# Probabilities' parts in four narrower buffers with products a step later, a shifted ring of accumulators, one gate multiplication on GpSimd, and closing scalings by pairs, in a two-layer encoder trunk

## The chip, the cores and the metric

The kernel runs on one core of a Trainium2 chip. The core has TensorE (PE: matrix products into the banks of PSUM, and transposes, which are products with an identity), VectorE (DVE), ScalarE (ACT), GpSimd (POOL) and SyncE (SP, which here issues DMAs). Each works through its own list of instructions in order and waits on semaphores for the others. The metric is the device time of one execution in microseconds (us), smaller is better.

## The reference

One sequence of 1024 tokens on a grid of 16 rows of 64, width 1024, passes two layers, all in float32:

```python
for l in range(DEPTH):
    h = rmsnorm(x, norm_gain[l])
    mk, mv = jnp.split(memn @ w_mem_kv[l], 2, axis=-1)
    ...
    if l % 2 == 0:
        qa, ka, va, qb, kb, vb, qm, gate = split_cols(h @ w_in_even[e], SPLIT_EVEN)
        ya = global_gqa(...); yb = window_gqa(...); ym = memory_attn(...)
        x = x + (concat(ya, yb, ym) * silu(gate)) @ w_out_even[e]
    else:
        qc, kc, vc, qm, gate = split_cols(h @ w_in_odd[o], SPLIT_ODD)
        yc = neighborhood_attn(qc, kc, vc, rpb_c[o])
        ym = memory_attn(qm, mk, mv)
        x = x + (concat(yc, ym) * silu(gate)) @ w_out_odd[o]
return rmsnorm(x, final_norm_gain)
```

The change lies in the odd layer, but for one line of the first stage. There 16 neighbourhood heads of 64 channels attend to the keys of a few grid rows around a query's own (at most three blocks of 128 keys for a block of 128 queries), four memory heads of 128 channels to 256 memory tokens; the heads' outputs are multiplied by a gate, go through one output projection, are added to x, and a last RMS norm closes.

## The kernel before

[...]

*Stages.* The projection of the global heads' queries and keys (0 to 143 us of the profile); the even layer's attention and output projection and the odd layer's first projections (to 985); the odd layer's memory heads (to 1124); its neighbourhood heads, called near below (to 1368); the output projection with the last norm (to 1490). Tiles of SBUF come from rings: each tag has a number of buffers, and a new tile takes the place of the oldest of its tag, for which the writer waits until the old one's last reader is done. The same holds for PSUM banks (pj, tr, s, pv, sa).

*Order.* In the odd layer the order of PE's instructions is that in which the code writes them. On the other engines a scheduler puts each instruction as early as its inputs allow, by priorities that the code gives by kind (`ahead`); `issue_after` holds one back behind another.

*First stage.* `project_a` begins with nine warm-up products into one bank of the tag pj, a ring of five that the projections then use. After the last of them the first scores (bank sa) of the memory heads follow; DVE adds the last projection's halves into q (L128).

*Memory heads of the odd layer.* `mem_flips` transposes a head's probabilities into two banks; `p_parts` makes of each the high part ph by a copy on ACT and the low part pl by a subtraction on DVE (L541), both of 512 columns; `mem_pv` takes three products for each. ph and pl have three buffers each.

*Near heads.* `near` runs over 128 steps n, one for each of 16 heads and 8 blocks. A step's score is two products on PE (s), a sum with the bias and a maximum on DVE (L1111), exp on ACT (L1114), a reciprocal on DVE (L1115) and the normalisation on POOL (L1116, tile pn). At every second step two key blocks, n-6 and n-5, are transposed (`flips`: PE into a bank tr, then `p_parts` of up to 384 columns). `values(n - 7)` takes the product of one key block's ph and pl with v into the accumulators pv. Between these, `fill` takes 1930 columns' worth of products from a list: the projections of keys and gates still to come, and at the end the first part of the output projection. POOL also makes the weight parts for that (L1276 for the output projection). The output of a pair of heads is done every 16 steps; `gated_steps` (which also takes the last memory head, at the start) then spreads its gating over the following scores, one job of POOL or DVE behind a score's normalisation, and only behind scores at which no weight job is left: the second half's multiplication (L477), the first half's (L480), and for the rows that have k of 6 or more a store, a load and three subtractions on POOL (L496, L498, L501). The last pair's jobs come after the loop, when the output projection has begun (`behind_held`).

*Output projection.* The rows y and their differences are loaded again as operands; its weights are split by ACT and POOL (L1276), and for each output block six products of a kind follow.

*The end.* `finish` works on the last 512 columns in two halves: residual, squares and their sums over channels by PE, the root (DVE), its spread to rows by PE, then for eight channel blocks the scaling by row and gain: three on POOL (L1488; gains applied before), five on DVE in one instruction each with the gain, and four stores per half.

## Time and profile before

| | |
|---|---|
| median of 3 runs | 1495.13 us (1492.85 to 1495.61) |
| the profiled execution | 1492.08 us |
| its span, first to last instruction | 1490.3 us |
| granted clock, mean | 0.998 |
| PE busy | 1468.7 us, 99% of the span |
| DVE, ACT, POOL busy | 1036.9, 832.0 and 634.7 us |
| PE's last work | about 1483 us |

In the lines of the profile each row has a start and a length in us, the engine, the line of the code (L62 stands for all that goes through `Pinned`, and is told apart by its tiles), the operation, and out<-in. A matmul's end is modelled, and neighbouring ones overlap; the starts tell the rate. In square brackets stands idle time ahead of a row and what ended it. Rows of a stage table hold start and end, length, and busy time (with instructions) of PE, PE's weight loads, DVE, ACT and POOL, then the granted clock, the share of the DMA engines and GB/s.

### The profile page before, as it was taken

The numbers are of one execution on the slowest core, as the hardware profiler recorded it, in microseconds if no ns is written. First come the engines' busy times: TensorE is split into PE (matmuls) and PEld (weight loads), VectorE is DVE, ScalarE is ACT, GpSimd is POOL, SyncE is SP. The second block draws the span as 40 slices with busy tenths as digits, with TensorE's granted clock in tenths as the row PEclk, the third lists the DMA queues.
The fourth block names the chain that finished last, engine by engine and source line by source line (L and its number), as shares of the span: only waits on it lengthen the run. The fifth ranks groups of instructions, "written<-read, shape, count | busy, mean of one in ns | idle before, by whom it ended". The sixth has DMA issues, their size and how long they took to land.

```text
span 1490.3 us, 25353 instructions
## 1 busy us (share of the span) xinstructions
PE 1468.7 (99%) x8385; PEld 1272.7 (85%) x8385; DVE 1036.9 (70%) x2121; ACT 832.0 (56%) x1855; POOL 634.7 (43%) x761
## 2 busy tenths in 40 slices
PE   9999999999999999999999999999999999999997
PEld 8898888988888788888879877888988888888886
DVE  6786777677676578776677766654346877788674
ACT  7743665656655456654545444444446777676452
POOL 1223668556765746543450000002325556664354
PEclk9999999999999999999999999999999999999999
DMA  8966335434433424388653444567675578689834
GB/s 285 317 157 184 112 119 174 128 107 137 127 125 129 139 87 135 98 285 292 196 178 114 138 138 142 154 164 262 212 259 166 181 216 249 207 295 341 305 101 140
DMA packets 173859, 271.90 MB, mean 182 GB/s; under 512 B 15648, under 2 KB 96800, under 8 KB 172704
## 3 DMA queue, kind: packets, MB, share of 16 engines
q1 hardware_dynamic: 173296, 270.20, 56.4%
q8 instruction: 66, 1.08, 0.3%
q14 instruction: 65, 0.53, 0.1%
q10 hardware_dynamic: 432, 0.09, 0.0%
HBM read 174.28 MB, written 83.89 MB: 173 GB/s over the span
## 4 chain that ended last, share of the span: by engine, by line
PE 84%; DVE 6%; DMA 5%; issue 2%; ACT 2%; POOL 1%; SPq 0%; POOLq 0%; DVEq 0%; ACTq 0%
PE pj L241 15%; PE pj L62 11%; PE x L1599 6%; PE tr L132 5%; PE pv L1063 4%; PE y L1599 4%; PE pv L62 3%; PE s L62 3%; PE pj L1329 3%; PE tr L62 2%; PE sa L1329 2%; PE pv L1599 2%; PE s L1329 2%; PE sa L1030 2%; PE sa L1031 2%
## 5 line engine op out<-in xcount | busy, mean ns | idle before, releaser
L241 PE MATMUL pj<-H,wh 128*128 128x512 f32 x704 | 233.6, 412 | 0.5 <-DVE vt L312 0.2
L541 DVE TENSOR_TENSOR pl<-tr,ph 128x512 fp32r<-128x512 f32 (+2 forms) x336 | 202.2, 615 | 42.6 <-ACT ph L124 40.4
L124 ACT ACTIVATE ph<-tr 128x512 fp32r<-128x512 f32 (+2 forms) x336 | 174.3, 539 | 97.1 <-PE tr L132 80.5
L157 POOL TENSOR_SCALAR wh<-wraw 128x512 fp32r<-128x512 f32 x48 | 33.3, 696 | 277.7 <-PE x L1599 235.1
L124 ACT ACTIVATE wh<-wraw 128x384 fp32r<-128x384 f32 (+1 forms) x163 | 89.0, 554 | 107.6 <-PE pj L1329 13.4
L241 PE MATMUL pj<-H,wl 128*128 128x512 f32 x352 | 139.3, 396 | 0.0
L241 PEld LDWEIGHTS pj<-H,wh 128*128 128x128 f32 x704 | 120.8, 190 | 19.1 <-POOL wh L157 0.6
L62 PE MATMUL pj<-H,wh 128*128 128x512 f32 x384 | 121.0, 396 | 0.0
L1116 POOL TENSOR_SCALAR pn<-pn,st 128x384 f32<-128x384 f32 (+1 forms) x128 | 72.6, 568 | 113.1 <-DVE st L1115 67.5
L132 PE MATMUL tr<-ident,P 128*128 128x128 f32 x752 | 115.5, 273 | 0.9 <-DVE pl L541 0.6
L1276 POOL TENSOR_TENSOR wl<-wraw,wh 128x384 fp32r<-128x384 f32 x56 | 63.6, 1137 | 97.0 <-ACT wh L124 87.5
L1114 ACT ACTIVATE pn<-pn,st 128x384 f32<-128x384 f32 (+1 forms) x128 | 75.2, 588 | 40.7 <-DVE st L1111 40.0
L132 PEld LDWEIGHTS tr<-ident,P 128*128 128x128 f32 x752 | 88.9, 140 | 9.1 <-DVE pl L541 1.5
L1036 ACT ACTIVATE P<-sa,st 128x1024 f32<-128x1024 f32 x64 | 71.5, 1117 | 35.3 <-PE tr L132 19.1
L1038 POOL TENSOR_SCALAR P<-P,st 128x1024 f32<-128x1024 f32 x64 | 74.6, 1168 | 32.2 <-DVE st L1037 32.2
L1035 DVE TENSOR_REDUCE st<-sa 128x1 f32<-128x1024 f32 x64 | 77.6, 1218 | 8.5 <-PE sa L1031 8.0
L62 PE MATMUL s<-k,q 128*128 128x384 f32 (+1 forms) x352 | 81.3, 327 | 0.0
L241 PEld LDWEIGHTS pj<-H,wl 128*128 128x128 f32 x352 | 66.3, 188 | 15.3
L62 PE MATMUL pj<-H,wl 128*128 128x512 f32 x192 | 75.8, 395 | 0.0
L159 POOL TENSOR_TENSOR wl<-wraw,wh 128x512 fp32r<-128x512 f32 x52 | 68.6, 1323 | 9.5 <-ACT wh L124 6.6
L62 PEld LDWEIGHTS pj<-H,wh 128*128 128x128 f32 x384 | 67.0, 189 | 5.8
L848 PE MATMUL pj<-ah,H 128*128 128x256 f32 x384 | 70.5, 282 | 0.9 <-ACT H L124 0.9
(559 smaller groups left out, 4171.2 us busy)
## 6 DMA issues: line engine op xcount, KB each, us to landing
wraw<-w_o SPq DMA_DIRECT2D x52, 256.0 KB, 3.7
y<-yb SPq DMA_DIRECT2D x24, 512.0 KB, 3.5
wraw<-s SPq DMA_DIRECT2D x64, 192.0 KB, 3.7
wraw<-w_e SPq DMA_DIRECT2D x44, 256.0 KB, 3.3
k<-k SPq DMA_DIRECT2D x42, 256.0 KB, 5.1
s<-bias SPq DMA_DIRECT2D x56, 192.0 KB, 2.0
wq<-w_o SPq DMA_DIRECT2D x40, 256.0 KB, 3.3
y<-sg SPq DMA_DIRECT2D x18, 512.0 KB, 2.9
```

Source lines behind the costliest of these rows:

```text
L62: return lambda *a, **k: self.tc.keep_in_program_order(getattr(self.engine, name)(*a, **k))
L124: return self.nc.scalar.activation(out, in_, AF.Copy, scale=scale)
L132: self.turned = self.fence = self.pe.transpose(o, i, self.ident)
L241: self.pe.matmul(a[:, :n], s[:, kt % UNIT, :], m, start=(kt == 0 and i == 0), stop=(kt == KT - 1 and i == 2))
L541: self.low = nc.vector.tensor_tensor(pl[:, :n], tr[:, :n], ph[:, :n], op=OP.subtract)
L1035: nc.vector.tensor_reduce(st[:, 0:1], s, axis=AX.X, op=OP.max, negate=True)
L1036: nc.scalar.activation(pt, s, AF.Exp, bias=st[:, 0:1], accum_out=st[:, 1:2])
L1038: self.normal = nc.gpsimd.tensor_scalar(pt, pt, st[:, 2:3], 0.5, op0=OP.mult, op1=OP.mult)
L1114: nc.scalar.activation(o, o, AF.Exp, bias=st[:, 0:1], scale=-1.0, accum_out=st[:, 2:3])
L1116: self.normal = normal = nc.gpsimd.tensor_scalar(o, o, st[:, 3:4], 0.5, op0=OP.mult, op1=OP.mult)
L1329: last = nc.tensor.matmul(bank, s[:, k, :], y[3 * u + k][m][:, cols], start=start and u + k + e == 0, stop=u == 1 and k + e == 4, skip_gro ...
L1599: self.last = nc.tensor.matmul(bank, ws[s][:, k, :], b[k][m], start=start and k + i == 0, stop=k == UNIT - 1 and i == 2, skip_group_check= ...
```

## The change

- In the odd layer ph and pl get four buffers instead of three, each of 384 columns instead of 512. The memory heads' parts are made in two pieces of 256 columns, with six products instead of three.
- The near heads' `values` come one step later after their transposes (n-8 for n-7), the loop is one step longer, and the load of the next v moves from step 7 to step 8 of a pair.
- Of the two gate multiplications of a near pair, the second half's goes from DVE to POOL. Nine jobs have a `gap` of 2, the last memory head's and those of the eight pairs of near heads: eight of the instructions are issued within the loop, the last pair's behind it.
- The warm-up's products use two pj banks in turn, by which every later tile of this tag takes the next bank of its ring.
- In `finish` the gains of the channel blocks that DVE scaled are applied early, by copies on ACT; the scalings are then products of two operands, two channel blocks at a time, and the stores come in the order of the pairs 2, 3, 0, 1. Squares of the output projection take the buffers of the tag bm in place of ph.

```diff
@@ -86,2 +86,3 @@
         self.raws = []
+        self.wide, self.square_tag = 512, "ph"
         self.later_jobs = ()
@@ -476,6 +477,6 @@
             yield
-        (nc.vector if gap > 1 else nc.vector).tensor_tensor(y[:, second], y[:, second], sg[:, second], op=OP.mult)
+        (nc.gpsimd if gap > 1 else nc.vector).tensor_tensor(y[:, second], y[:, second], sg[:, second], op=OP.mult)
         for _ in range(gap):
             yield
-        (nc.vector if gap > 1 else nc.vector).tensor_tensor(y[:, first], y[:, first], sg[:, first], op=OP.mult)
+        nc.vector.tensor_tensor(y[:, first], y[:, first], sg[:, first], op=OP.mult)
         if k < 6:
@@ -536,4 +537,4 @@
         nc = self.nc
-        ph = self.st("ph", [128, 512], F32R)
-        pl = self.st("pl", [128, 512], F32R)
+        ph = self.st("ph", [128, self.wide], F32R)
+        pl = self.st("pl", [128, self.wide], F32R)
         with self.ahead("part"):
@@ -659,3 +660,4 @@
             self.flip((tr[c][:, b * 128:(b + 1) * 128], pt[:, b, c * 128:(c + 1) * 128]) for c in range(2) for b in range(4))
-        return [self.p_parts(t, 512) for t in tr]
+        n = min(512, self.wide // 256 * 256)
+        return [[self.p_parts(t[:, i:i + n], n) for i in range(0, 512, n)] for t in tr]
 
@@ -663,6 +665,7 @@
         vh, vl = (kv[:, i, :].rearrange("p (c d) -> p c d", c=2)[:, c, :] for i in (2, 3))
-        ph, pl = parts
+        n = 512 // len(parts)
         with self.ahead("pv"):
-            for e, (a, b) in enumerate(((vh, ph), (vl, ph), (vh, pl))):
-                self.pe.matmul(o, a, b, start=c + e == 0, stop=c * e == 2)
+            for i, (ph, pl) in enumerate(parts):
+                for e, (a, b) in enumerate(((vh, ph), (vl, ph), (vh, pl))):
+                    self.pe.matmul(o[:, i * n:(i + 1) * n], a, b, start=c + e + i == 0, stop=c * e == 2, skip_group_check=True)
 
@@ -964,5 +967,5 @@
         nc.scalar.activation(self.rs_m, warm.bitcast(F32)[:, :2], AF.Sqrt)
-        p = self.ps("pj")
+        p = [self.ps("pj") for _ in range(2)]
         for i in range(9):
-            nc.tensor.matmul(p, warm[:, :128], warm, start=True, stop=True)
+            nc.tensor.matmul(p[i % 2], warm[:, :128], warm, start=True, stop=True)
         w0, w1m = io["w_mem0"], io["w_mem1"]
@@ -1156,3 +1159,3 @@
 
-        for n in range(128 + 7):
+        for n in range(128 + 8):
             for f in (n - 6, n - 5) if n % 2 == 0 else ():
@@ -1177,3 +1180,3 @@
                     pair["q"] = load_q(j + 1)
-                if j < 7 and at == 7:
+                if j < 7 and at == 8:
                     pair["v"] = load_v(j + 1)
@@ -1185,6 +1188,6 @@
                     pair[j]["g"] = gate(j, ("sg", "mk")[j % 2])
-            if n >= 7:
-                values(n - 7)
-                if (n - 7) % 16 == 15:
-                    j = (n - 7) // 16
+            if n >= 8:
+                values(n - 8)
+                if (n - 8) % 16 == 15:
+                    j = (n - 8) // 16
                     self.later_jobs.append(self.gated_steps(pair[j]["g"], pair[j]["y"], yd, ROWS.index(j), 2))
@@ -1357,3 +1360,3 @@
 
-            sq = self.st("ph" if k else "vt", [128, 512])
+            sq = self.st(self.square_tag if k else "vt", [128, 512])
             nc.scalar.activation(sq, x, AF.Square)
@@ -1456,5 +1459,8 @@
         at = [xs[k // 2][:, k % 2, :] for k in range(KT)]
-        for k in range(3):
-            nc.gpsimd.tensor_scalar(at[k], at[k], gains[k], 1.0, op0=OP.mult, op1=OP.mult)
-        sq = self.st("ph", [128, 512])
+        for k in range(7):
+            if k < 3:
+                nc.gpsimd.tensor_scalar(at[k], at[k], gains[k], 1.0, op0=OP.mult, op1=OP.mult)
+            else:
+                self.copy(at[k], at[k], gains[k])
+        sq = self.st(self.square_tag, [128, 512])
         ss, rows = [self.ps("pv")[:, :16] for _ in range(2)], {}
@@ -1486,11 +1492,22 @@
             self.copy(sb, rows[h][1])
-            for k in range(3):
-                nc.gpsimd.tensor_tensor(at[k][:, c], at[k][:, c], sb, op=OP.mult)
-            for k in (4, 5, 6, 7, 3):
-                pinned.scalar_tensor_tensor(at[k][:, c], at[k][:, c], gains[k], rows[h][0], op0=OP.mult, op1=OP.mult)
+            two = lambda t: t[:, None, :].to_broadcast([128, 2, c.stop - c.start])
+            out = lambda p: nc.sync.dma_start(
+                self.io["out"][2 * p:2 * p + 2, :, 512 + c.start:512 + c.stop].rearrange("k p t -> p k t"), xs[p][:, :, c])
+            x = xs[0][:, :, c]
+            nc.gpsimd.tensor_tensor(x, x, two(sb), op=OP.mult)
+            if h == 0:
+                nc.gpsimd.tensor_tensor(at[2][:, c], at[2][:, c], sb, op=OP.mult)
+            for p in (2, 3):
+                x = xs[p][:, :, c]
+                pinned.tensor_tensor(x, x, two(rows[h][0]), op=OP.mult)
                 yield
-                if k % 2:
-                    for p in (k // 2,) if k > 3 else (0, 1):
-                        nc.sync.dma_start(self.io["out"][2 * p:2 * p + 2, :, 512 + c.start:512 + c.stop].rearrange("k p t -> p k t"),
-                                          xs[p][:, :, c])
+                out(p)
+            if h == 0:
+                pinned.tensor_tensor(at[3][:, c], at[3][:, c], rows[h][0], op=OP.mult)
+            else:
+                x = xs[1][:, :, c]
+                pinned.tensor_tensor(x, x, two(rows[h][0]), op=OP.mult)
+            yield
+            out(0)
+            out(1)
 
@@ -1499,2 +1516,3 @@
             nc.scalar.activation(sq[:, c], x3[:, c], AF.Square)
+            self.copy(x3[:, c], x3[:, c], gains[7])
         cols = [slice(0, 256), slice(256, 512)]
@@ -1860,4 +1878,5 @@
             self.alias = {"P": "k"}
-            with self.phase("l1", ("pool", "pool"), q=4, k=8, v=2, pn=8, ph=3, pl=3, sg=1, yb=2, bt=1, vt=3, bm=2,
+            with self.phase("l1", ("pool", "pool"), q=4, k=8, v=2, pn=8, ph=4, pl=4, sg=1, yb=2, bt=1, vt=3, bm=2,
                             p_s=2, p_tr=2, p_pv=2, p_pj=2):
+                self.wide, self.square_tag = 384, "bm"
                 first, begun = self.odd(wo, kvd[1], yd[1], vd, mqd, qd, gd)
```

PE, at the end of the near stage, where `fill` has no products left: the last transposes (tr), and the products of key blocks 125 and on (pv). Before:

```order
L62 MATMUL tr_3530_16274<-ident_1_63,pn_3493_16146 128x128
L62 MATMUL tr_3530_16274<-ident_1_63,pn_3506_16182 128x128
L62 MATMUL tr_3530_16274<-ident_1_63,pn_3510_16199 128x128
L62 MATMUL tr_3533_16282<-ident_1_63,pn_3506_16182 128x128
L62 MATMUL tr_3533_16282<-ident_1_63,pn_3510_16199 128x128
L62 MATMUL pv_3513_16206<-ph_3527_16259,v_3326_15544 128x384
L62 MATMUL pv_3513_16206<-pl_3528_16260,v_3326_15544 128x384
L62 MATMUL pv_3513_16206<-ph_3531_16278,v_3326_15544 128x384
L62 MATMUL pv_3513_16206<-pl_3532_16279,v_3326_15544 128x384
L62 MATMUL pv_3513_16206<-ph_3534_16285,v_3326_15544 128x256
L62 MATMUL pv_3513_16206<-pl_3535_16286,v_3326_15544 128x256
```

After, from the last row of block 126's transposes:

```order
L62 MATMUL tr_3562_16380<-ident_1_63,pn_3542_16307 128x128
L62 MATMUL tr_3565_16388<-ident_1_63,pn_3539_16293 128x128
L62 MATMUL tr_3565_16388<-ident_1_63,pn_3542_16307 128x128
L62 MATMUL pv_3551_16337<-ph_3557_16362,v_3368_15687 128x128
L62 MATMUL pv_3552_16338<-ph_3557_16362,v_3368_15687 128x256
L62 MATMUL pv_3551_16337<-pl_3558_16363,v_3368_15687 128x128
L62 MATMUL pv_3552_16338<-pl_3558_16363,v_3368_15687 128x256
L62 MATMUL pv_3552_16338<-ph_3560_16370,v_3368_15687 128x384
L62 MATMUL pv_3552_16338<-pl_3561_16371,v_3368_15687 128x384
L62 MATMUL pv_3552_16338<-ph_3563_16384,v_3368_15687 128x384
L62 MATMUL pv_3552_16338<-pl_3564_16385,v_3368_15687 128x384
```

Before, a block's products follow straight on the transposes of the last two; now the four products of the block before these (128 and 256 columns) stand between.

POOL, in the output projection, where the last pair is gated: yb is the pair's output, mk its gate and later its differences, wl the low parts of weights. Before:

```order
L501 TENSOR_TENSOR yb_3305_15480<-sg_3320_15522,yb_3305_15480 128x512
L1276 TENSOR_TENSOR wl_3562_16391<-wraw_3560_16388,wh_3561_16390 128x384
L1276 TENSOR_TENSOR wl_3574_16454<-wraw_3572_16451,wh_3573_16453 128x384
L1276 TENSOR_TENSOR wl_3580_16486<-wraw_3578_16483,wh_3579_16485 128x384
L496 TENSOR_TENSOR mk_3491_16133<-yb_3428_15925,mk_3491_16133 128x512
L498 TENSOR_TENSOR mk_3491_16133<-yb_3428_15925,mk_3491_16133 128x512
L501 TENSOR_TENSOR yb_3428_15925<-mk_3491_16133,yb_3428_15925 128x512
```

After:

```order
L502 TENSOR_TENSOR yb_3338_15591<-sg_3353_15633,yb_3338_15591 128x512
L1279 TENSOR_TENSOR wl_3595_16504<-wraw_3593_16501,wh_3594_16503 128x384
L1279 TENSOR_TENSOR wl_3607_16567<-wraw_3605_16564,wh_3606_16566 128x384
L478 TENSOR_TENSOR yb_3461_16036<-yb_3461_16036,mk_3523_16239 128x512
L1279 TENSOR_TENSOR wl_3613_16599<-wraw_3611_16596,wh_3612_16598 128x384
L497 TENSOR_TENSOR mk_3523_16239<-yb_3461_16036,mk_3523_16239 128x512
L499 TENSOR_TENSOR mk_3523_16239<-yb_3461_16036,mk_3523_16239 128x512
L502 TENSOR_TENSOR yb_3461_16036<-mk_3523_16239,yb_3461_16036 128x512
L1279 TENSOR_TENSOR wl_3619_16633<-wraw_3617_16630,wh_3618_16632 128x384
```

The multiplication (L478 of the new code) now stands between two weight parts, and the pair's three subtractions behind one weight part more; in the loop the other multiplications stand each behind a normalisation (L1116), with a normalisation following. On PE the low part that follows, which had two products of the next bank ahead of it, now has seven.

DVE, at the end, from the first half's scalings on: tr holds the row of roots, H and yb are the pairs of channel blocks. Before:

```order
L62 SCALAR_TENSOR_TENSOR yb_3549_16324<-yb_3549_16324,gain_2_65,tr_3764_17411 128x256 x2
L62 RECIPROCAL rq_v_3767_17426<-pv_3759_17351 128x2
L62 SCALAR_TENSOR_TENSOR pv_3759_17351<-pv_3759_17351,rq_v_3767_17426 128x2 x2
L62 SCALAR_TENSOR_TENSOR rq_y_3768_17427<-pv_3759_17351,rq_v_3767_17426 128x2
L62 SCALAR_TENSOR_TENSOR yb_3550_16325<-yb_3550_16325,gain_2_65,tr_3764_17411 128x256 x2
L62 SCALAR_TENSOR_TENSOR H_3544_16319<-H_3544_16319,gain_2_65,tr_3764_17411 128x256
L62 SCALAR_TENSOR_TENSOR yb_3549_16324<-yb_3549_16324,gain_2_65,tr_3769_17433 128x256 x2
L62 SCALAR_TENSOR_TENSOR yb_3550_16325<-yb_3550_16325,gain_2_65,tr_3769_17433 128x256 x2
L62 SCALAR_TENSOR_TENSOR H_3544_16319<-H_3544_16319,gain_2_65,tr_3769_17433 128x256
```

After:

```order
L62 TENSOR_TENSOR yb_3582_16437<-yb_3582_16437,tr_3797_17530 128x2x256
L62 TENSOR_TENSOR yb_3583_16438<-yb_3583_16438,tr_3797_17530 128x2x256
L62 RECIPROCAL rq_v_3800_17545<-pv_3792_17468 128x2
L62 SCALAR_TENSOR_TENSOR pv_3792_17468<-pv_3792_17468,rq_v_3800_17545 128x2 x2
L62 SCALAR_TENSOR_TENSOR rq_y_3801_17546<-pv_3792_17468,rq_v_3800_17545 128x2
L62 TENSOR_TENSOR H_3577_16432<-H_3577_16432,tr_3797_17530 128x256
L62 TENSOR_TENSOR yb_3582_16437<-yb_3582_16437,tr_3802_17552 128x2x256
L62 TENSOR_TENSOR yb_3583_16438<-yb_3583_16438,tr_3802_17552 128x2x256
L62 TENSOR_TENSOR H_3577_16432<-H_3577_16432,tr_3802_17552 128x2x256
```

Scalings by one block (twice 128x256) have become one of 128x2x256; two of them, instead of two single ones, stand ahead of the second half's reciprocal.

## The prediction

> **What bounds the kernel now.** I read the page's head first, then busy time by stage, then who waits for whom in the near stage, then the places themselves in order of time.
>
> ```profile
> span 1490.3 us, 25353 instructions
> PE 1468.7 (99%) x8385; PEld 1272.7 (85%) x8385; DVE 1036.9 (70%) x2121; ACT 832.0 (56%) x1855; POOL 634.7 (43%) x761
> ...
> 1124.00:1368.00 244.00, 240.89 (x1413) 212.17 (x1412) 191.60 (x598) 176.59 (x460) 140.26 (x193) 1.00 0.73 236
> 1368.00:1483.00 115.00, 113.78 (x535) 94.10 (x534) 74.43 (x118) 54.35 (x105) 54.39 (x48) 1.00 0.56 186
> 1483.00:1490.30 7.30, 0.30 (x3) 0.06 (x1) 2.66 (x7) 0.38 (x1) 2.80 (x5) 0.56 0.79 276
> ```
>
> TensorE (PE) is busy nearly always and the granted clock is 1.00 in the near stage (1124 to 1368), so only time in which PE waits can be won, and the 7.3 us after its last work. In the near stage DVE works 191.6 of 244 us and POOL 140.3, so neither is full. The run of this profile took 1492.08 us; the median of the timed runs is 1495.13, which is 3.05 more. I make the sum against the former and carry the difference over to the latter.
>
> ```profile
> PEld pv L62 <- DVE pl L541: 6.4, 12, 0.9
> PE pv L62 <- DVE pl L541: 2.8, 8, 0.6
> ...
> 1276.98 0.34 PE L62 MATMUL pv<-ph,v 128*128 128x384 f32 x1
> 1277.16 0.34 PE L62 MATMUL pv<-pl,v 128*128 128x384 f32 x1
> ...
> 1278.38 0.34 PE L62 MATMUL pv<-ph,v 128*128 128x384 f32 x1
> 1278.69 0.89 DVE L541 TENSOR_TENSOR pl<-tr,ph 128x384 fp32r<-128x384 f32 x2
> 1279.30 0.44 PE L62 MATMUL pv<-pl,v 128*128 128x384 f32 x1 [0.58 <-DVE pl L541]
> ```
>
> The first two lines are waits of the near stage: total, times, longest. The product with the low part pl waits for VectorE (DVE) to make it. PE's own 2.8 us understates this, since a matmul's modelled end covers part of the gap: undisturbed, the second product starts 0.18 us after the first (1276.98, 1277.16), here 0.92 us after (1278.38, 1279.30). That is 0.74 lost where the row says 0.58. The weight loads' 6.4 us in 12 waits is the better sum, and I use it.
>
> **The change, part by part.**
>
> *Values one step later, parts in four buffers.* One step is a score, a fill and a product: 244 us over 135 steps, 1.8 us. Today the even key blocks' parts are wanted one step after their transposes, the odd ones' two; the change makes it two and three. The longest wait is 0.9 us, half of the step given. In DVE's new order every pl stands behind the same score's work as before, none behind a later one, so the step is real slack. Four buffers hold the block more that lives; a buffer comes free the same number of steps before its next use as now, so no wait comes with it. The load of the next v moves a step with the values; no row has PE waiting for v.
>
> The end of the stage is different, because there the fill is used up:
>
> ```profile
> 1364.75 0.71 PE L62 MATMUL tr<-ident,pn 128*128 128x128 f32 x5
> 1365.47 0.34 PE L62 MATMUL pv<-pl,v 128*128 128x384 f32 x1
> 1365.94 0.44 PE L62 MATMUL pv<-ph,v 128*128 128x384 f32 x1
> 1366.12 0.89 DVE L541 TENSOR_TENSOR pl<-tr,ph 128x384 fp32r<-128x384 f32 x2
> 1366.73 0.44 PE L62 MATMUL pv<-pl,v 128*128 128x384 f32 x1 [0.35 <-DVE pl L541]
> ```
>
> From 1365.94 to 1366.73 are 0.79 us for a product of 0.18, from 1365.47 to 1365.94 are 0.47: 0.9 lost in all. The new order puts only block 124's four products between, about 0.45 us by the 128- and 256-column starts. So of 6.4 us I take 5.5 in the body as gone, and of the 0.9 at the end 0.4: **-5.9** (bounds -6.7, the same waits counted from start to start, and 0).
>
> *Parts of 256 columns in the memory heads.* 48 products of 512 columns become 96 of 256.
>
> ```profile
> 1042.93 0.63 PE L62 MATMUL pv<-ph,k 128*128 128x512 f32 x2
> 1043.40 0.39 PE L62 MATMUL pv<-pl,k 128*128 128x512 f32 x1
> ...
> 1474.31 0.28 PE L1329 MATMUL pj<-H,wl 128*128 128x256 f32 x1
> 1474.43 0.39 PE L1329 MATMUL pj<-H,wh 128*128 128x256 f32 x2
> ```
>
> Two 512-column products take 0.47 us from start to start, one of 256 takes 0.12: 0.235 against 0.24. That is 48 x 0.005, **0.2** at most, and I take 0: no wait of PE for these parts is listed in this stage, and the 16 more copies and subtractions lie on ACT and DVE, which have room. Below nothing it can't be.
>
> *The accumulators' ring in the first stage.* Each projection still follows the one five before it, so inside that stage nothing moves. The warm-up ends before the first operands are there. But the bank that the last projection leaves changes hands at the stage's end:
>
> ```profile
> 142.00 0.39 PE L1031 MATMUL sa<-k,q 128*128 128x512 f32 x1
> 142.55 0.68 DVE L128 TENSOR_TENSOR q<-pj,q 128x512 fp32r<-128x512 f32 x1
> 143.38 0.47 PE L1030 MATMUL sa<-k,q 128*128 128x512 f32 x1 [0.99 <-DVE q L128]
> ```
>
> Now the second score's bank is read by DVE until 143.23. In the new order this score has no wait on DVE, and the projection after it has. Four score products of 0.23 us fit between (142.23 to 143.16), so 0.2 us of the wait is left: **-0.8** (bounds -1.0 and 0).
>
> *One gate multiplication of two on GpSimd.* Nine multiplications leave DVE, eight inside the stage's loop and that of the last pair behind it.
>
> ```profile
> L1116 POOL TENSOR_SCALAR pn<-pn,st 128x384 f32<-128x384 f32 x96 | 56.8, 593 | 82.4 <-DVE st L1115 41.6 <-PE tr L62 26.5 <-PE s L62 9.2
> L496 POOL TENSOR_TENSOR sg<-yb,sg 128x512 f32<-128x512 f32 x3 | 3.9, 1288 | 0.0
> ...
> L477 DVE TENSOR_TENSOR yb<-yb,mk 128x512 f32<-128x512 f32 x5 | 3.7, 735 | 0.0
> ```
>
> On GpSimd I price one like L496, 1.29 us against DVE's 0.74. Queued behind it are the next block's normalisation (L1116) and, for it, PE's transposes four steps later (7 us). GpSimd sits idle 82 us ahead of 96 of its normalisations, 0.86 us each, and never more than one such job is given out per score, so the eight fall where no weight job stands: **0** (bounds 0 and 8 x 1.29 = 10.3).
>
> [...]
>
> ```profile
> 1374.85 0.68 DVE L128 TENSOR_TENSOR q<-q 128x512 fp32r<-128x512 f32 x1
> 1376.27 1.20 POOL L1276 TENSOR_TENSOR wl<-wraw,wh 128x384 fp32r<-128x384 f32 x1 [2.98 <-ACT wh L124]
> 1376.52 1.50 DVE L128 TENSOR_TENSOR q<-q 128x512 fp32r<-128x512 f32 x1
> ```
>
> The same subtraction takes 0.68 us alone and 1.50 beside a GpSimd subtraction. [...]
>
> *The last pair's multiplication* stands on GpSimd in line with weight parts of the output projection, and behind it a store, a load and three subtractions.
>
> ```profile
> 1376.16 0.32 SPq L491 DMA_DIRECT2D y<-yb  x1
> 1383.97 1.29 POOL L496 TENSOR_TENSOR mk<-yb,mk 128x512 f32<-128x512 f32 x1 [2.07 <-issue]
> 1388.05 2.76 POOL L1276 TENSOR_TENSOR wl<-wraw,wh 128x384 fp32r<-128x384 f32 x2
> ...
> 1391.21 0.40 PE L1342 MATMUL pv<-k,wl 128*128 128x512 f32 x1
> ```
>
> It can start when the weight part of 1376.27 is done, 1377.5, and ends at 1378.8, so the store goes 2.6 us late and the three subtractions too. The weight part behind them is then ready at about 1392.0 instead of 1389.4, where PE wants it at 1391.21. But the new order lets PE do five products more of the next bank first (1.2 us), so it is wanted at 1392.4. I take **+0.3** (bounds 0 and 2.6).
>
> *The closing scalings.*
>
> ```profile
> 1366.93 1.28 DVE L1354 TENSOR_TENSOR H<-H,pj 128x512 f32<-128x512 f32 x2
> ...
> 1480.94 0.87 DVE L62 SCALAR_TENSOR_TENSOR yb<-yb,gain,tr 128x256 f32<-128x256 f32 x2 [0.64 <-PE tr L132]
> 1481.62 4.27 POOL L1488 TENSOR_TENSOR H<-H,vt 128x256 f32<-128x256 f32 x6 [8.49 <-ACT vt L124]
> 1481.77 0.17 DVE L62 RECIPROCAL rq_v<-pv 128x2 f32<-128x2 f32 x1
> 1485.76 1.01 SPq L1494 DMA_DIRECT2D out<-H  x2
> ...
> DMA  0000000000399306999999999999999998000000
> ```
>
> GpSimd's six of 0.71 become two of 1.29 and one of 0.71: 3.3 us for 4.3. DVE's two scalings ahead of the second half's root take 1.28 instead of 0.87, so that root starts 0.4 us later; the three pairs behind it end at about 1485.5, where DVE and GpSimd end at 1485.7 and 1485.9 now. The gains move to ACT, which the stage table shows busy for 54 of the last stage's 115 us, as four copies of 512 columns and two of 256, each behind its square. The last row (40 slices of 1480 to 1490.4) says what sets the end: the DMA engines work on a first store in slices 10 to 13 (from 1482.6), have a hole, and are full from slice 15 to slice 33 (1483.9 to 1488.8): seven stores of equal size in 4.85 us, 0.69 us each. The hole of 0.5 us (a third full, empty, 0.6 full) mostly goes if the second store is issued at 1482.3 instead of 1483.05, as it would be, with DVE's first pair done. **-0.4** (bounds -0.7 and +0.4, the late root).
>
> Squares in two buffers: one square per product of 4.2 us, its sum 1.3 us; 0.
>
> Sum: -5.9 - 0.8 + 0 + 0 + 0.3 - 0.4 = **-6.8 us**, 1485.3 for the profiled run and 1488.3 for the median.
>
> **The rivals.**
>
> *The wait moves to the transposes.* A transpose needs a bank that pl frees. At the stage's end this is so (five transposes at 1364.75, just as DVE ends the parts before them), and one step more for the values gives the banks nothing. If it holds in the body too, some 5 of the 5.9 us come back: 1493.3. Against it: no line names PE's transposes of pn as waiting.
>
> [...]
>
> *The last pair's chain costs all of it.* 2.6 us once at the weight part, and as much again where the late store is loaded back: -6.8 - 0.3 + 5.2 = -1.9, 1493.2.
>
> *It doesn't do what it says*: if DVE made each pl a step later too, nothing would be won. Its order says no.
>
> **How the numbers follow.** 0.67 for the forecast, 0.13 for the transposes, 0.09 for the last pair's chain, 0.09 for GpSimd, 0.02 for the last. A measurement of this kernel can tell about 0.2%, 3.0 us. The forecast lies beyond it, two rivals within, one above: faster 0.70, same 0.18, slower 0.12. The range goes down to all good ends, -1.0 - 6.7 - 0.7 = -8.4, less another 1.7 for the spread of the runs shown (2.8 us): 1485. Up it takes in both rivals at 1493 and a part of GpSimd's: 1496.
>
> **What would show it.** Right: the waits of pv for pl in the near stage fall from 6.4 us to under 1; the wait of sa near 143 is gone; DVE's L477 rows stand on POOL at about 1.29 us. Wrong: PE's tr waits for pl or for pn from POOL; the wl of 1388 comes after PE wants it; stores that end later than now after PE's last work.

## The result and the profile after

Over seven runs of each the changed kernel took 1488.59 us (1485.98 to 1491.39), the one before 1494.25 us (1491.65 to 1495.66). The ratio is 0.9965 with a 95% interval of 0.9952 to 0.9978: 5.2 us faster (3.3 to 7.2). A second set of runs gave 0.9971 (0.9959 to 0.9984). The profiled execution took 1488.59 us, 3.5 less than that of before. The head of the profile's page, and the stage table at the same times as before:

```profile
span 1486.8 us, 25511 instructions
PE 1467.6 (99%) x8433; PEld 1274.7 (86%) x8433; DVE 1030.7 (69%) x2124; ACT 837.2 (56%) x1877; POOL 644.2 (43%) x767
...
1124.00:1368.00 244.00, 242.70 (x1432) 215.88 (x1432) 190.28 (x596) 178.46 (x466) 148.82 (x202) 1.00 0.73 238
```

POOL works 8.6 us more in this window and DVE 1.3 less. A sharper measure is the time between the same two instructions of PE, the near stage's first score of 384 columns and its last product with pl. Rows of the timeline, before and then after:

```profile
1123.03 0.51 PE L62 MATMUL s<-k,q 128*128 128x384 f32 x2
...
1367.13 0.32 PE L62 MATMUL pv<-pl,v 128*128 128x256 f32 x1
```

```profile
1124.51 0.51 PE L62 MATMUL s<-k,q 128*128 128x384 f32 x2
...
1364.01 0.32 PE L62 MATMUL pv<-pl,v 128*128 128x256 f32 x1
```

That is 244.1 us before and 239.5 after: 4.6 won in this stage. Who waits for whom in it (total, times, longest):

```profile
PE tr L62 <- DVE pl L542: 0.9, 2, 0.6
```

And three of its places in the timeline:

```profile
1279.00 0.34 PE L62 MATMUL pv<-ph,v 128*128 128x384 f32 x1
1279.18 0.34 PE L62 MATMUL pv<-pl,v 128*128 128x384 f32 x1
...
1296.76 0.52 PE L62 MATMUL tr<-ident,pn 128*128 128x128 f32 x3 [0.33 <-DVE pl L542]
...
1363.46 0.34 PE L62 MATMUL pv<-ph,v 128*128 128x384 f32 x1
1363.63 0.42 PE L62 MATMUL pv<-pl,v 128*128 128x384 f32 x1
```

No product waits for pl any more (the pair at 1279.00 is 0.18 us apart, where it was 0.92), and the waits listed for PE in this stage went from the products, 6.4 us by weight loads, to the transposes, 0.9 us (and 0.2 us for v). In the first stage the second score no longer stands before DVE is done with q:

```profile
143.63 0.40 PE L1033 MATMUL sa<-k,q 128*128 128x512 f32 x1
...
144.56 0.39 PE L1033 MATMUL sa<-k,q 128*128 128x512 f32 x1
144.89 0.68 DVE L129 TENSOR_TENSOR q<-pj,q 128x512 fp32r<-128x512 f32 x1
```

And the end of the kernel, first the timeline:

```profile
1478.23 1.28 DVE L62 TENSOR_TENSOR yb<-yb,tr 128x512 f32<-128x512 f32 x2 [0.64 <-PE tr L133]
1478.98 0.99 SPq L1494 DMA_DIRECT2D out<-yb  x2
1480.34 0.40 PE L133 MATMUL tr<-ident,rq_y 128*128 128x128 f32 x2 [1.59 <-DVE rq_y L62]
1480.58 0.38 PE L133 MATMUL pj<-ident,rq_y 128*128 128x128 f32 x2
```

Then the DMA engines' share in 40 slices of 0.26 us, from 1476.4 to 1486.8:

```profile
DMA  0000000000000499999999999999999999600000
```

The stores now run without a hole, from 1479.8 to 1485.4. PE waits 1.6 us for the second root instead of 1.2. From the near stage's last product to PE's last start are 116.7 us (115.9 before), and from there to the end of the span 6.1 (7.3 before).

The table shows three stretches of each kernel's profiled execution: the near stage as above; from there to PE's last start; from that to the end of the span. The ratio is to runs of the kernel before on the same chip.

| kernel | near | output projection | end | ratio (95%) |
|---|---|---|---|---|
| before | 244.1 | 115.9 | 7.3 | |
| changed | 239.5 | 116.7 | 6.1 | 0.9965 (0.9952 to 0.9978) |
| changed, again (e9) | 239.2 | 116.6 | 5.8 | 0.9971 (0.9959 to 0.9984) |
| products at n-7 again (e1) | 243.1 | 116.4 | 6.1 | 0.9989 (0.9980 to 0.9997) |
| both multiplications on DVE (e2) | 240.9 | 116.3 | 6.1 | 0.9971 (0.9963 to 0.9980) |
| both on GpSimd (e3) | 246.2 | 117.0 | 5.8 | 1.0008 (0.9995 to 1.0022) |
| buffers and later products alone (e4) | 241.9 | 115.9 | 7.2 | 0.9978 (0.9966 to 0.9990) |
| gating earlier (e5) | 245.6 | 117.7 | 5.8 | 0.9989 (0.9975 to 1.0004) |
| both on GpSimd and earlier (e6) | 239.6 | 117.0 | 6.1 | 0.9969 (0.9958 to 0.9980) |
| earlier, root first (e7) | 243.2 | 117.2 | 7.0 | 1.0005 (0.9994 to 1.0017) |
| earlier but for one pair (e8) | 238.7 | 116.7 | 6.1 | 0.9967 (0.9953 to 0.9981) |
| that, last pair on DVE (e10) | 239.3 | 116.3 | 6.1 | 0.9964 (0.9950 to 0.9978) |

### The profile page after: what moved, and what is told of

Its sections match the earlier page's. It is cut to its first block, busy times and chain, and to the rows that moved or that the text cites. A ratio compares the mean times of both kernels' runs of the same rounds, so it can differ in the third digit from the quotient of the medians.

```text
span 1486.8 us, 25511 instructions
## 1 busy us (share of the span) xinstructions
PE 1467.6 (99%) x8433; PEld 1274.7 (86%) x8433; DVE 1030.7 (69%) x2124; ACT 837.2 (56%) x1877; POOL 644.2 (43%) x767
## 4 chain that ended last, share of the span: by engine, by line
PE 86%; DMA 6%; DVE 3%; ACT 2%; issue 1%; SPq 1%; POOL 1%; POOLq 0%; ACTq 0%; DVEq 0%
PE pj L242 16%; PE pj L62 11%; PE x L1617 6%; PE tr L133 6%; PE pv L1066 4%; PE y L1617 4%; PE pv L62 3%; PE s L62 3%; PE pj L1332 3%; PE tr L62 3%; PE sa L1332 2%; PE pv L1617 2%; PE sa L1033 2%; PE s L1332 2%; PE sa L1034 2%; PE pj L851 2%
## 5 line engine op out<-in xcount | busy, mean ns | idle before, releaser
L160 POOL TENSOR_TENSOR wl<-wraw,wh 128x512 fp32r<-128x512 f32 x52 | 69.6, 1341 | 10.3 <-ACT wh L125 7.8
```

## The experiments

The first four expectations count the near stage from a later start, a projection product some 9 us on, to the end of its last product: 234.8 us before (from 1132.61), 231.4 after (from 1132.94). In what follows the table's count is used, and the differences are what is compared; where an expectation gives a length of the stage, its own count stands beside it.

**The later products undone (e1).**

```diff
-        for n in range(128 + 8):
+        for n in range(128 + 7):
...
-                if j < 7 and at == 8:
+                if j < 7 and at == 7:
...
-            if n >= 8:
-                values(n - 8)
-                if (n - 8) % 16 == 15:
-                    j = (n - 8) // 16
+            if n >= 7:
+                values(n - 7)
+                if (n - 7) % 16 == 15:
+                    j = (n - 7) // 16
```

> The changed kernel with values at n-7 again (and the load of v at step 7); four buffers, 256-column parts, the ring, the multiplication on GpSimd and the closing scalings stay as changed. Theory (the later products make the gain of the near stage): the stage from its first projection product to its last product with pl, 231.4 us in the changed kernel's profile and 234.8 before, goes back to 234 to 236, the waits of PE for pl in it are back at 5 to 7 us counted on the weight loads, and the time is 3 to 6 us longer than that of the changed kernel, a ratio to before of 0.999 to 1.001. Rival (the relief of DVE by GpSimd made the gain): the stage stays at 231 to 232 and the ratio at 0.9965.

The stage is 3.6 us longer (in the expectation's count 233.8 us, just short of its 234) and the time 0.9989 of before, at the lower edge of the theory's range and far from the rival's 0.9965. The waits are back, about as many and as long as before:

```profile
PEld pv L62 <- DVE pl L542: 5.9, 12, 0.8
...
PE pv L62 <- DVE pl L542: 2.6, 7, 0.5
```

What is left of the gain with the products at n-7 (243.1 against 244.1) is 1.0 us: the larger part needs the later products.

**Both multiplications on DVE (e2), and both on GpSimd (e3).**

```diff
-        (nc.gpsimd if gap > 1 else nc.vector).tensor_tensor(y[:, second], y[:, second], sg[:, second], op=OP.mult)
+        nc.vector.tensor_tensor(y[:, second], y[:, second], sg[:, second], op=OP.mult)
```

> The changed kernel with both gate multiplications on DVE. Theory (the eight cost nothing and bring nothing, the last pair's costs 0 to 0.3 us): ratio to before 0.9965 within 0.0015, stage 231 to 232 us. Rival 1 (GpSimd's multiplications hold normalisations): 3 us or more faster than the changed kernel, stage 229 or less. Rival 2 (they made the gain by relieving DVE): 3 us slower, waits of transposes or products for pl above 3 us.

```diff
-        nc.vector.tensor_tensor(y[:, first], y[:, first], sg[:, first], op=OP.mult)
+        (nc.gpsimd if gap > 1 else nc.vector).tensor_tensor(y[:, first], y[:, first], sg[:, first], op=OP.mult)
```

> The changed kernel with the first half's multiplication on GpSimd as well: eight more of 1.29 us in the near stage. Theory (GpSimd's idle time takes them): stage 231 to 232.5 us, ratio to before 0.9960 to 0.9985; only the last pair's, with its store another 1 to 2.6 us later, may cost up to 1 us. Rival (each holds a normalisation and with it PE): 8 x 1.29 = 10 us longer at the most, a ratio of 1.000 to 1.004, with waits of PE's transposes for pn.

With both on DVE the time can't be told from the changed kernel's (0.9971 against 0.9965 and 0.9971), so neither rival holds. But the profile has the stage 1.4 to 1.8 us longer than in the changed kernel's two profiles (232.8 us in the expectation's count, above its 231 to 232), nearly all of it ahead of transposes:

```profile
DVE yb L1158 <- DMA y<-yb: 5.3, 3, 2.1
...
PE tr L62 <- DVE pl L542: 2.4, 4, 1.4
```

With both on GpSimd the theory fell: 246.2 us, 6.7 more (238.1 in the expectation's count), and slower than the changed kernel by 0.43% or some 6 us. The ratio, 1.0008, lies in the rival's range; the rival's mechanism isn't there, for PE doesn't wait for normalisations:

```profile
DVE yb L1158 <- DMA y<-yb: 6.1, 3, 3.9
...
PE s L62 <- DMA k<-k: 2.6, 3, 1.0
...
PE tr L62 <- DVE pl L542: 2.3, 2, 1.8
```

DVE waits for a store. A pair's output tile yb has two buffers; the sum that closes a head (L1158) writes into the one that the pair before the last is stored from, and stands on DVE until that store has landed. Behind it on DVE stand pl, and behind these PE's transposes, for which a bank must come free. The changed kernel has the same row with 3.7 us in 3 waits. These transposes cost 2.7 us from start to start, at one place (1303.59). More, 3.7 us, was lost at another, where the last key pair's loads came late: PE stood about 2.2 us for them (the second row), and then the granted clock was low: 0.89 over the 15 us of the stage table, where the changed kernel has 1.00. The table:

```profile
1330.00:1345.00 15.00, 13.18 (x68) 11.38 (x67) 9.18 (x31) 8.17 (x22) 7.85 (x10) 0.89 1.04 350
```

**Buffers and later products alone (e4).** This is the kernel before with four buffers, the 256-column parts and the products at n-8.

> The kernel before with the four buffers of 384 columns, the 256-column parts and the products one step later alone; both multiplications on DVE, the old ring and the old closing scalings. Theory: the near stage's 3.4 us come with this alone, a ratio to before of 0.9970 to 0.9985, and the wait of sa for q (1.0 us) is there again. Rival (buffers and lag need DVE's relief): ratio 0.999 to 1.000.

The ratio, 0.9978, is as expected, but the stage is not: it is 2.2 us shorter than before where the changed kernel's is 4.6 (in the expectation's count 1.0 of the 3.4). It is also 1.0 us longer than in e2, which has the same code in this stage; e4's profile has waits of PE for v, 1.3 us, that e2's has not. So two profiles of one code can lie 1 us apart here. e4's profile has the old end (115.9, and 7.2 us behind PE) and the old wait in the first stage, which none of the kernels with the shifted ring has:

```profile
PE sa L1033 <- DVE q L129: 1.0, 1, 1.0
```

**The gating two scores earlier (e5), and this with both multiplications on GpSimd (e6).** If the chain behind the multiplications is what comes late, it can be started earlier.

```diff
-        for _ in range(gap):
-            yield
+        yield
         (nc.gpsimd if gap > 1 else nc.vector).tensor_tensor(y[:, second], y[:, second], sg[:, second], op=OP.mult)
-        for _ in range(gap):
-            yield
+        yield
         nc.vector.tensor_tensor(y[:, first], y[:, first], sg[:, first], op=OP.mult)
```

> The changed kernel with one score instead of two ahead of each of a pair's two gate multiplications, so that everything behind them (store, load, subtractions, last store) comes earlier by up to two scores. Theory (what is left of PE's waits in the near stage starts with DVE's write into yb, which waits 3.7 us in 3 waits for the store of the pair before the last, and with it the pl behind it): these waits fall below 1 us, PE's waits of tr for pl from 0.9 to under 0.3, the stage from its first 384-column score to its last product with pl is 238 to 239 us against 239.5, and the time is 0.5 to 1.5 us shorter, a ratio to before of 0.9950 to 0.9965. Rival (the transposes wait because two banks are too few): the waits of yb fall and those of tr stay, the stage is 239.5 and the ratio 0.9965.

> Both multiplications on GpSimd, and both one score earlier each. With both on GpSimd the near stage took 246.2 us, 6.7 more than in the changed kernel. Theory (what costs is the lateness of the chain behind the multiplications: the store that holds SyncE's queue, and yb's buffer): the stage goes back to 240 to 243 us and the ratio to before to 0.997 to 0.999. Rival (it is GpSimd's own time, 8 x 1.29 us that hold normalisations): the stage stays at 245 to 247 us, the ratio at 1.0008.

The second of these answers the question for GpSimd: 16 multiplications in the stage, started earlier, take 239.6 us and 0.9969. The stage is even a little under the expected 240 to 243. So GpSimd's own time is not what cost 6 us in e3; it is when the chain behind the multiplications comes. With this order PE has no wait for k and no slow clock in the stage.

The first went wrong: slower than the changed kernel (0.9989), 245.6 us. Of what the theory names, a part came. Against the changed kernel 0.5 us are won at the transposes of 1296.76; at those of 1326.68 the first three come 0.6 us earlier, but the next three wait for a pl of their own, and nothing is left. DVE's wait for the store is 1.8 us instead of 3.7 (below 1 was expected), and the transposes' waits for pl stay at 1.0 in the list (under 0.3 was expected). A new wait, once, cost more than all that was won. PE's timeline there:

```profile
1326.69 0.52 PE L62 MATMUL tr<-ident,pn 128*128 128x128 f32 x3 [0.49 <-DVE pl L540]
1330.46 0.55 PE L62 MATMUL s<-k,q 128*128 128x256 f32 x1 [3.25 <-DMA k<-k]
```

The stage table of the same place (granted clock third from the right):

```profile
1326.60:1330.40 3.80, 0.52 (x3) 0.31 (x3) 2.19 (x7) 2.18 (x7) 2.00 (x3) 0.85 1.03 230
1330.40:1334.00 3.60, 3.07 (x9) 2.52 (x10) 0.60 (x3) 0.60 (x2) 3.13 (x4) 0.50 1.03 199
1334.00:1337.00 3.00, 3.00 (x12) 2.54 (x11) 0.73 (x3) 0.71 (x2) 1.67 (x3) 0.65 1.03 378
```

And SyncE's queue:

```profile
1318.24 0.32 SPq L490 DMA_DIRECT2D y<-yb  x1
1318.61 0.75 SPq L491 DMA_DIRECT2D mk<-y  x1
1319.46 0.73 SPq L366 DMA_DIRECT2D k<-k  x1
```

In the changed kernel three of the four loads of keys came first:

```profile
1320.07 0.47 SPq L366 DMA_DIRECT2D k<-k  x1
...
1324.60 0.40 SPq L492 DMA_DIRECT2D y<-yb  x1
1325.09 0.47 SPq L367 DMA_DIRECT2D k<-k  x1
1325.61 1.32 SPq L493 DMA_DIRECT2D mk<-y  x1
```

PE stood 3.5 us, counted from start to start, for the last key pair, whose four transfers (L366, L367) came behind a store and a load of 0.5 MB each; from issue to landing they took a median of 12.0 us instead of 5.8, with the DMA engines full (share 1.03). Then PE went on at a granted clock of 0.50 for 3.6 us and of 0.65 for 3.0; by the granted clocks of the two rows behind the stall it lost about 2.8 us more (3.6 x 0.50 + 3.0 x 0.35, an estimate).

**One pair left out (e8), and the changed kernel beside it (e9).** The sixth pair's gating, whose store it was, keeps its two scores, and so does the last memory head's at the start of the stage. The new argument is their number (0: as `gap`).

```diff
-    def gated_steps(self, sg, y, yd, k, gap=1):
+    def gated_steps(self, sg, y, yd, k, gap=1, lead=0):
...
-        for _ in range(gap):
+        for _ in range(lead or gap):
...
-        for _ in range(gap):
+        for _ in range(lead or gap):
...
-                    self.later_jobs.append(self.gated_steps(pair[j]["g"], pair[j]["y"], yd, ROWS.index(j), 2))
+                    self.later_jobs.append(self.gated_steps(pair[j]["g"], pair[j]["y"], yd, ROWS.index(j), 2, 2 if j == 5 else 1))
```

> The gating two scores earlier for all near pairs but the sixth, whose store and load stood ahead of the last key pair's four loads on SyncE's queue. Theory (that kernel lost its gain, and more, by this alone: the keys landed late, PE stood 3.5 us and then ran at half its clock): no wait of PE for k, the granted clock 1.00 from 1320 to 1345 us, the near stage from its first 384-column score to its last product with pl 238 to 239.3 us (239.5 in the changed kernel, 245.6 with all pairs earlier), a ratio to before of 0.9955 to 0.9970. Rival (earlier gating loads the DMA engines everywhere): the wait for k stays or moves to another pair, stage over 242, ratio 0.998 or more.

> The changed kernel once more, for a comparison with the others of this call: a ratio to before of 0.9952 to 0.9978, the near stage within 0.5 us of 239.5.

The wait for the keys is gone and the clock is full, in the same stretch of time:

```profile
1326.60:1330.40 3.80, 3.47 (x22) 2.73 (x21) 2.62 (x11) 2.23 (x7) 0.81 (x3) 1.00 1.02 267
1330.40:1334.00 3.60, 3.60 (x22) 3.16 (x22) 2.71 (x10) 2.67 (x9) 2.24 (x4) 1.00 1.01 360
```

So with this one pair's chain put back, and its store and load behind three of the keys' loads again, what the earlier gating lost is gone. The stage takes 238.7 us, 0.5 to 0.8 less than in the changed kernel's profiles; the time (0.9967 against 0.9971 beside it) can't tell that from nothing.

**The end (e7), and the last pair (e10).** In e7 the second half's root goes ahead of the second closing pair; in e10 the last pair's multiplication is on DVE, and the sixth pair has three scores.

```diff
         one = scale(0)
         next(one)
-        next(one)
         list(root(1))
```

> As the kernel with the gating two scores earlier, and at the end the second half's root stands on DVE behind one closing pair instead of two. Theory (the late root costs PE 0.4 us, but the stores, which the DMA engines then work off without a hole, set the end): PE's wait of tr for rq_y falls from 1.6 to about 1.0 us, the time from PE's last work to the end grows by as much as PE is done earlier or more, and the ratio is that of the kernel without it within 0.0010. Rival (the root is on the path): the end comes 0.4 us earlier, too small for the time, but to be seen as a shorter stretch from the near stage's last product to the end of the span, under 122.3 us (122.8 in the changed kernel).

> As the kernel with the sixth pair excepted, with one score more ahead of that pair's multiplications so that all four loads of the last keys go first, and with the last pair's multiplication, the one behind the loop, on DVE. Theory (that one on GpSimd costs 0.4 us in the output projection): from the near stage's last product to PE's last work 116.2 to 116.4 us against 116.7; near stage 238 to 239.3; a ratio of 0.9950 to 0.9968, 0.3 to 1.5 us under the changed kernel. Rival (the stretch varies by as much from run to run): 116.6 or more.

With the root first, PE waits 1.2 us for it and is done 0.5 us earlier than in e5, but the second store is issued at 1483.11 instead of directly behind the first, the hole is back, and the end comes 7.0 us behind PE instead of 5.8. SyncE's queue, and the DMA strip from 1480 to 1490.2:

```profile
1481.87 0.39 SPq L1492 DMA_DIRECT2D out<-yb  x1
...
1483.11 0.39 SPq L1492 DMA_DIRECT2D out<-H  x1
```

```profile
DMA  0000000000099701999999999999999999700000
```

So the stores set the end, as the theory says; by these profiles the order with the late root is the better one. e7's ratio, 1.0005, lies further from e5's 0.9989 than I had expected, with intervals that overlap. In e10 the output projection took 116.3 us, as in the other kernel with the last pair on DVE (e2), against 116.7, 116.6 and 116.7 with it on GpSimd (changed, e9, e8). That looks like 0.3 to 0.4 us, but it is not the multiplication's price: e1, with it on GpSimd, has 116.4. From the near stage's last product to the first sums over the second half's squares (`pv<-inv_d`), just ahead of the closing, are 112.55 and 112.56 us with it on DVE (e2, e10); with it on GpSimd 112.96 and 112.54 in the changed kernel's two profiles, 112.88 in e8 and 112.63 in e1. One program lies as far apart as the two engines do, which is what the rival said of the stretch; e9's 116.6 comes from behind this point (4.1 us to PE's last start, 3.7 in the changed kernel's first profile). The ratio of e10, 0.9964, is no better than the changed kernel's by what can be measured. Nothing tried beats the changed kernel clearly.

## Why the prediction was right, and where not

The time came out at 1488.59 where 1488.3 was forecast; against the runs of before beside it the gain is 5.2 us where the sum said 6.8. That the two times lie so close is luck: the gain fell short, and the runs of before beside it are faster by 0.9 us than those that the forecast started from (1494.25 for 1495.13). The profiled stretches, without the stages that the change doesn't touch, give -4.6 - 1.0 + 0.4 + 0.8 - 1.2 = -5.6. The two profiled executions differ by less, 3.5 us, since the changed kernel's has a longer first stage: its first score of the memory heads comes at 143.63 us, that of before at 141.30, and over all twelve profiles this start lies anywhere from 140.49 to 143.76.

- *Later products, -5.9.* The mechanism is right: 6.4 us of waits of the products are gone, and undoing this part alone brings 3.6 us and the waits back. The term was too large: the stage won 4.6 in all, this part alone brought 2.2 (e4), and undone it cost 3.6, though 5.9 us of the weight loads' waits came back with it. What the prediction gave as a rival happened in part: some of the waiting moved to the transposes, at two places with 0.33 and 0.58 us by their rows, 0.5 and 0.8 from start to start. A transpose there waits for the bank that pl frees, as the rival put it, and pl comes late because DVE stands for the store of yb. The changed kernel at 1326.68, and then the row that before already had, which the prediction doesn't show:

```profile
1324.98 0.68 DVE L1158 TENSOR_TENSOR yb<-pv,bt 64x512 f32<-64x512 f32 x1 [1.26 <-DMA y<-yb]
...
1326.12 0.88 DVE L542 TENSOR_TENSOR pl<-tr,ph 128x256 fp32r<-128x256 f32 x2
...
1326.68 0.98 PE L62 MATMUL tr<-ident,pn 128*128 128x128 f32 x6 [0.58 <-DVE pl L542]
```

```profile
DVE yb L1155 <- DMA y<-yb: 3.2, 2, 2.1
```

  Started earlier, the chain to that store gives back 0.5 to 0.8 us of the stage (e8). The list of e8 still has 0.9 us of transposes waiting for pl, and a third bank was not tried, so how much is the store's and how much the banks' stays open.
- *The stage's end.* The last 384-column products (1363.46) follow each other undisturbed; from the last score to the last product are 8.2 us against 8.9. Of the 0.9 lost there 0.7 are won, where 0.4 was counted; the changed kernel's second profile (e9) has 8.7, so only 0.2.
- *256-column parts, 0.* From the last product of the stage ahead to the near stage's first score are 105.8 us before and 106.2 in most of the others (106.3 in the changed kernel's first profile): +0.4, twice the "at most" that was worked out from starts, and still small.
- *The ring, -0.8.* The wait of 1.0 us is gone in every kernel with the shift and there in the one without. The scores follow each other at 0.23 us, so the 0.2 that should have stayed is 0 here.
- *One multiplication on GpSimd, 0.* In time nothing, as forecast. The bounds, 0 and 10.3, left out a gain without a reason: the profiles have the stage 1.4 to 1.8 us longer with it on DVE, little more than the 1 us by which two profiles of one code differ. Whether it is a gain, and why, is not settled; shorter work on DVE and an earlier store would both do it. No run shows a multiplication that holds a normalisation and PE with it, which the range's upper end and 0.09 of the chances count: with twice as many (e3) none of PE's waits in the stage is for one. What GpSimd cost was the lateness of what is queued behind it: 246.2 us in e3, and 239.6 with the same multiplications a score earlier each (e6). Beside GpSimd single instructions of DVE took longer. The prediction's rows have a subtraction at 0.68 us alone and at 1.50 beside one on GpSimd; the changed kernel has a multiplication, in the list of one line's instructions and in the timeline:

```profile
L481 DVE TENSOR_TENSOR yb<-yb,sg x5: 680/683/1373, 638.6 to 1352.5; 128x512 f32<-128x512 f32 x5
```

```profile
1305.93 1.30 POOL L464 TENSOR_TENSOR wl<-wraw,wh 128x512 fp32r<-128x512 f32 x1
1306.41 1.37 DVE L481 TENSOR_TENSOR yb<-yb,sg 128x512 f32<-128x512 f32 x1
```

  The first half's multiplication takes 683 ns (median of five), and 1373 beside a weight part's subtraction on GpSimd. In the changed kernel's list of waits none of DVE's in this stage ends with the moved multiplication (in e1 one does, of 1.1 us).
- *The last pair, +0.3.* The working gives no such cost: the weight part is ready at 1392.0 there and wanted at 1392.4. The profiles show none either that can be told from the differences of one program (112.54 and 112.96 us, against 112.55 with it on DVE), and PE has no wait for the low part in its list. The stretch grew by 0.8 us, of which 0.4 is the late root of the next item; the rest is within those differences.
- *The closings, -0.4.* PE's late root costs the 0.4 that was given as a bound, and the end behind PE is 1.2 shorter: -0.8, beyond the bound of -0.7. The step that failed set the late root against the gain at the end. With the DMA engines full from the first store on (share 1.06 from 1479.8 to 1485.4), it costs nothing: the first store's issue and the volume set the end, and e7 shows the opposite choice to be worse (7.0 us behind PE for 5.8 in e5).

## What to carry to other kernels

Time a wait by its whole chain: giving a consumer one more step took away all that it waited for (6.4 us), and the next releaser in the queue of the same engine (here a store that frees a tile) decided what was left. Before moving work to an idle engine, ask what is queued behind it there and on the DMA issuer; here its own microseconds cost nothing that shows (16 multiplications, 239.6 us in e6 against 239.5), while the order of a few transfers cost six (245.6 in e5). With the DMA engines as full as there (share 1.03), keep what PE needs next ahead of stores that are wanted later.

## What the runs showed of the hardware

*A slow clock can follow a stall of PE.* After PE had stood 3.5 us in e5, the granted clock was 0.50 for 3.6 us and 0.65 for the next 3.0. In slices of half a us the clock falls at about 1329.3, 2.1 us after PE's last transposes ended, and is full again at about 1336.1, 5.6 us after PE's next start; the stage table's 0.85 ahead of the 0.50, and 0.65 behind it, come to the same. Elsewhere a slow clock came behind a shorter stall. In the changed kernel's second profile (e9), in the even layer, which the change doesn't touch, PE went from a start at 223.21 to 225.23 without a new product, and then ran at 0.55 (the timeline, and a row of the stage table):

```profile
223.21 0.39 PE L242 MATMUL pj<-H,wl 128*128 128x512 f32 x1
...
225.23 1.84 PE L133 MATMUL tr<-ident,P 128*128 128x128 f32 x4 [1.64 <-POOL P L655]
```

```profile
226.20:230.00 3.80, 3.68 (x10) 2.82 (x11) 1.81 (x2) 1.12 (x2) 3.72 (x5) 0.55 0.36 107
```

The length of the stall doesn't decide it alone, though. Seven of the twelve profiles have this wait at this place; in five of them the clock is low behind it (e2, e3, e6, e8, e9: 0.97 in each over 200 to 260 us), in two it is not (e1, e4: 1.00). And e1 has the longest gap of the seven, 2.4 us from start to start (223.94 to 226.35):

```profile
226.35 1.69 PE L133 MATMUL tr<-ident,P 128*128 128x128 f32 x4 [2.02 <-POOL P L655]
```

```profile
226.20:230.00 3.80, 3.27 (x14) 2.30 (x15) 1.23 (x2) 1.12 (x2) 3.72 (x7) 1.00 0.39 108
```

What decides is open.

*One program's profiles differ by such a place.* From start to start it cost 4.3 us in e9 against the changed kernel's first profile, where PE doesn't wait there and the clock stays at 1.00: 2.9 us of waiting and 1.4 of slow clock. In e1 it cost 3.3 us, all of it waiting. The lowest and the highest of the changed kernel's seven runs lie 5.4 us apart; whether that place is what makes the spread was not tried. A comparison of two whole profiles would have put it down to the change; the stretches between the same two instructions don't, though they too differ by up to 1 us from profile to profile.
